# The next layer's modulation steps moved out of the early gates into the background list

## The chip, the cores and the metric

The kernel runs on one core of one Trainium2 chip. The metric is the device time of one execution in microseconds; the time of a kernel is the median of several runs.

## The reference

The model is a trunk of two layers on 512 tokens of width 1024, in float32. Each layer first makes its modulation from the conditioning vector, then runs three token mixers side by side (MLA with 8 heads, a sliding window of 128 with 8 heads, and a differential attention with 4 heads), and merges them by sigmoid gates:

```python
mod = c_act @ w_ada[l] + b_ada[l]
shift, scale, gate = split_cols(mod, (D, D, D))
h = rms_norm(x, g_pre[l]) * (1.0 + scale) + shift
... = split_cols(h @ w_in[l], IN_SPLITS)
o_a, o_b, o_c = (mixer(...) * silu(z)) @ w_o      # MLA, sliding, differential
y = (g[0] * o_a + g[1] * o_b + g[2] * o_c) @ w_out[l]
x = x + gate * rms_norm(y, g_post[l])
```

`mod` does not depend on `x`. So the shift and scale of layer 1 can be computed at any time in layer 0, up to the point where layer 1's `h` is made, and the gate of a layer at any time up to its last line.

## The kernel before

All of the activations stay on the core, transposed (`hTh`, `hTl`: width on the partitions, 512 tokens along the free dimension). Each float32 operand is split into a high part and a remainder, and each product is three matmuls (`mm3`, L87 to L89). A weight block of 128 x 1024 is a unit (`wunit`): one load of 512 KB into `wr` (two buffers), the high part by ACT into `wh` (L81), the remainder by DVE into `wl` (L84), three buffers each. A unit gives 24 matmuls of 128x512 and an accumulator in the PSUM tag `dn` (two buffers).

A layer runs through these stages: MLA's inputs and its eight heads; the early gates (`gates_early`: six gate projections of the second mixer and five of the third, whose units are pulled forward so that their matmuls fill PE during MLA); keys, values and queries of the sliding attention (`swa_kv`, `swa_q`, with the evacuation at L807); the sliding attention (scores at L878 and L879, reductions at L880); four projections for z (`silu_z`); the first merge (eight steps, each with a gate projection and half a unit of `w_o_mla`); the differential attention, head by head (`diff_qkv`, z, scores at L952 and L953, reductions at L954), with the second merge's steps mixed in by `fill`; the third merge; and the output phase, in whose end `boundary_tok` makes the next layer's `h`. The helper `transposed_block` (L704) turns the softmax weights for the products with v.

The modulation of layer 1 is `mod_late`: four quarters of four steps each. A step loads two rows of 512 columns per partition (512 KB into a `wr` buffer, L245) and adds them into an accumulator `acc` with two vector operations (L248 for the first of a quarter, L251 for the others). When a quarter's four steps are through, four products with a column of ones sum the accumulator over the partitions (L257, in `dn`), and one or two small vector operations write `ashf` or `amul`. The gate row of the current layer is `mod_rows`: eight steps, each one load (L229) and one vector operation of 128x1024 (L232, L235). `gate_rows` uses the result at L298 to L302.

Where the steps stand in the program is set by two lists. `some(at)` is called in `gates_early` and `swa_q`; at the positions in `MPOS` it issues one of the first eight steps of `mod_late`. Of the positions, 5, 11 and 12 occur in `gates_early`; a loop after `swa_q` issues the five that are left. What remains of `mod_late`, and then `mod_rows`, is the generator `background`, from which `bg_step` takes one step at a time: after each of the four z projections (`ZBS` is 1), at the start of each step of the first two merges, and twice in each head's `diff_qkv`. `gate_rows` empties what is left.

The final order on each engine is not the program's. A planner orders each engine's queue by priority with modelled durations, where the program's place is the priority and `high_priority` moves instructions up (the units by `WOFF`, 4000 in the early gates and 2000 after them). Each engine then works its queue in that order and waits on semaphores. Buffers of a tag go round: a new tile waits until an older one of its tag is released. The accumulators of the first two quarters take buffers of `u` (eight, shared with the split outputs of the mixers), the other two take `big` (eight).

Of the kernel before, what the change touches and what calls it, by code (L numbers as in the profile page):

```python
# [17 lines left out]
P = 128  # L18
S = 512
# [31 lines left out]
def hybrid_kernel(ctx, tc, x, c, w_ada, b_ada, g_pre, g_post, w_in, g_q, w_uq, g_kv, w_ukv,  # L51
# [11 lines left out]
    def T(tag, shape, dt=F32, bufs=None):  # L63
        count[0] += 1
        return sb.tile(shape, dt, tag=tag, name=f"{tag}_{count[0]}",
                       bufs=bufs or BUFS.get(tag, 1))
# [6 lines left out]
    def Q(tag):  # L73
        count[0] += 1
        return ps.tile([P, S], F32, tag=tag, name=f"ps_{tag}_{count[0]}", bufs=PB[tag])
# [10 lines left out]
    def mm3(o, ah, al, bh, bl, start, stop):  # L86
        pe.matmul(o, ah, bh, start=start, stop=False)  # L87
        pe.matmul(o, ah, bl, start=False, stop=False)  # L88
        pe.matmul(o, al, bh, start=False, stop=stop)  # L89
# [3 lines left out]
    @contextmanager  # L93
    def behind(*ins):
        with ExitStack() as es:
            for i in ins or fence:
                es.enter_context(tc.issue_after(i.ins))
            yield
# [3 lines left out]
    def wunit(parts, big=False):  # L102
        raw = T("wr", [P, 1024])
        h = T("big" if big else "wh", [P, 1024], F32R)
        lw = T("big" if big else "wl", [P, 1024], F32R)
        n = parts[-1][1]
        with tc.high_priority(offset=WOFF[0]):
            for lo, hi, src, shp in parts:
                dst = raw[:, lo:hi]
                if shp:  # L110
                    dst = dst.rearrange("p (a b) -> p a b", a=shp)
                units.append(sp.dma_start(out=dst, in_=src))
            with behind():
                act_copy(h[:, :n], raw[:, :n])
                sub(lw[:, :n], raw[:, :n], f(h[:, :n]))
        return h, lw
# [58 lines left out]
    def par(l, k, i=0, n=1):  # L175
        lo = k + l * PR_STEP[k] + i
        return prT[lo // 32][:, lo % 32:lo % 32 + n]
# [61 lines left out]
    def mod_late(l):  # L239
        for q in range(4):  # L240
            which, j = q // 2, 4 * (q % 2)
            acc = T("u" if q < 2 else "big", [P, S])
            for k in range(0, KT, 2):
                raw = T("wr", [P, 2, S])
                sp.dma_start(out=raw, in_=w_ada[l].rearrange("(p k) b -> p k b", k=KT)  # L245
                             [:, k:k + 2, q * S:(q + 1) * S])
                if k == 0:
                    dve.tensor_scalar(out=acc, in0=raw[:, 0], scalar1=cact[:, 0:1],  # L248
                                      scalar2=None, op0=ALU.mult)
                for i in range(k == 0, 2):  # L250
                    dve.scalar_tensor_tensor(out=acc, in0=raw[:, i],  # L251
                                             scalar=cact[:, k + i:k + i + 1], in1=acc,
                                             op0=ALU.mult, op1=ALU.add)
                yield
            pst = Q("dn")
            for i in range(4):
                pe.matmul(pst[:, i:i + 1], acc[:, i * P:(i + 1) * P], ones[:, 0:1],  # L257
                          start=True, stop=True)
            js = slice(j, j + 4)
            if which == 0:  # L260
                dve.tensor_tensor(out=ashf[l][:, js], in0=pst[:, 0:4],
                                  in1=par(l, PR_SHIFT, j, 4), op=ALU.add)
            else:
                dve.scalar_tensor_tensor(out=amul[l][:, js], in0=pst[:, 0:4], scalar=1.0,
                                         in1=par(l, PR_SCALE, j, 4),
                                         op0=ALU.add, op1=ALU.add)
                dve.tensor_tensor(out=amul[l][:, js], in0=amul[l][:, js],
                                  in1=par(l, PR_GPRE, j, 4), op=ALU.mult)
# [203 lines left out]
    def silu_z(l, col, hh, hl):  # L472
        zz = T("zz", [P, S])
        z = proj_T(l, col, hh, hl)
        return silu_of(zz, z)

    def silu_of(zz, z):
        act.activation(out=zz, in_=z, func=AF.Tanh, scale=0.5)
        dve.scalar_tensor_tensor(out=zz, in0=zz, scalar=1.0, in1=z, op0=ALU.add, op1=ALU.mult)  # L479
        return zz  # L480
# [17 lines left out]
    NC_LATE = 3  # L498
    FN = 1

    MPOS = (5, 6, 7, 8, 9, 10, 11, 12)
    ZBS = 1

    def gates_early(l, hh, hl, some):
        for j in range(NB_EARLY):
            d = dr.tile([P, S], F32, tag=f"gb{l}_{j}", name=f"gb{l}_{j}", bufs=1)
            early[l, 1, j] = d
            t = gate_tanh(l, 1, j, hh, hl)
            act.dma_start(out=d, in_=t)
            some(j)  # L510
        for j in range(NC_LATE, KT):
            d = dr.tile([P, S], F32, tag=f"gc{l}_{j}", name=f"gc{l}_{j}", bufs=1)
            early[l, 2, j] = d
            t = gate_tanh(l, 2, j, hh, hl)
            act.dma_start(out=d, in_=t)
            some(8 + j)
# [278 lines left out]
    def gate_u(o, zz):  # L795
        dve.scalar_tensor_tensor(out=o, in0=o, scalar=0.5, in1=zz, op0=ALU.mult, op1=ALU.mult)
        return split_u(o)
# [47 lines left out]
    def swa_q(l, hh, hl, some):  # L845
        qs = []
        for i in range(4):
            some(16 + i)
            qs += stack_q(l, C_QB + i * P, hh, hl)
        return qs  # L850
# [219 lines left out]
    def rest_of_layer(l, hh, hl, acc, za):  # L1070
        rest = None
        if l == 0:
            fence[:] = [amuls[-1]]
            wh, wl = wunit([(0, 1024, w_in[l][:, C_ZA + 3 * P:C_ZA + 4 * P]
                             .rearrange("(k p) c -> p k c", p=P), KT)])
            z3 = Q("dn")

            def part(lo, hi):
                for k in range(lo, hi):
                    mm3(z3, wh[:, k * P:(k + 1) * P], wl[:, k * P:(k + 1) * P], hh[:, k],  # L1080
                        hl[:, k], k == 0, k == KT - 1)

            def rest(t, ins):
                with behind(ins):
                    part(*ZR[t:t + 2])
                if t == NT - 1:
                    za.append(silu_of(T("zz", [P, S]), z3))

            part(0, ZR[0])
        else:  # L1090
            za = za + [silu_z(l, C_ZA + i * P, hh, hl) for i in range(4)]
        if l == 0:
            fence[:] = [amuls[2]]
        wts = {0: mla_pair_weights(l, 0, "ta")}
        cl, kp = mla_inputs(l, acc, rest)
        v = mla_v(l, cl)
        if l == 0:
            fence.clear()
        oa = mla_attention(l, cl, kp, v, wts)
        tables = [setup_bias()] if l == 0 else []  # L1100
        for t in tables:
            next(t)
        WOFF[0] = 4000
        fence.clear()
        late = mod_late(l + 1) if l + 1 < DEPTH else iter(())
        spread = [8]

        def table():
            if tables:
                try:  # L1110
                    tables[0].send(units[-1])
                except StopIteration:
                    tables.clear()

        def some(at):
            table()
            if at in MPOS and spread[0] > 0:
                spread[0] -= 1
                next(late, None)

        gates_early(l, hh, hl, some)
        WOFF[0] = 2000
        kk, vb = swa_kv(l, hh, hl)
        qs = swa_q(l, hh, hl, some)
        while spread[0] > 0:
            some(MPOS[0])
        for _ in range(12):
            table()
        ua = [gate_u(oa[i], za[i]) for i in range(4)]
        m = []  # L1130
        ob = swa_attention(l, qs, kk, vb)
        bg[:] = [background(l, late)]
        zb = []
        for i in range(4):
            zb.append(silu_z(l, C_ZB + i * P, hh, hl))
            bg_step(ZBS)
        ub = [gate_u(ob[i], zb[i]) for i in range(4)]
        merge(l, 0, w_o_mla, ua, hh, hl, m)
        mb = merge_steps(l, 1, w_o_swa, ub, hh, hl, m, None)
        od = diff_attention(l, hh, hl, lambda n: [next(mb) for _ in range(n)])  # L1140
        for _ in mb:
            pass
        t4 = gates_late(l, hh, hl)
        gg = gate_rows(l)
        return merge(l, 2, w_o_diff, od, hh, hl, m, t4=t4), gg

    hh, hl, acc, za = layer0_input()
    with behind(loads[-1]):
        setup_small()
    for l in range(DEPTH):  # L1150
        if l > 0:
            acc = acc4(True)
# [67 lines left out]
```

## Time and profile before

| | before |
|---|---|
| median of 3 runs | 1180.55 us (1180.5 to 1180.76) |
| the profiled execution's own time | 1178.78 us |
| its span, first to last instruction | 1176.7 us |
| PE busy | 1146.0 us, 97% |
| DVE busy | 844.2 us, 72% |
| ACT busy | 631.5 us, 54% |
| mean granted TensorE clock | 0.993 |

PE is TensorE's matmul queue, DVE VectorE, ACT ScalarE, POOL GpSimd, SP the engine that issues the loads (SPq where the issue itself is meant). A row of the waits gives the engine and line that waited, what it waited for, and the sum, count and longest in us. A row of the timeline gives start and duration in us, engine, line, operation, tiles and shapes; behind it stands the idle time before it, with what ended it. L12 is line 12 of the kernel.

### The profile page before, as it was taken

How to read it: one execution, taken by the hardware profiler on the slowest of the kernel's cores; microseconds unless marked ns; L12 is line 12 of the kernel's file. 1: busy time of each engine (PE TensorE's matmuls, PEld its weight loads, DVE VectorE, ACT ScalarE, POOL GpSimd, SP SyncE). 2: the span in 40 equal slices, each digit the busy share in tenths (PEclk: the TensorE clock that was granted, in tenths of full speed). 3: DMA queues.
4: the chain of work that ended last, by engine and by line, in shares of the span. 5: the costliest groups of instructions: out<-in, count | busy, mean ns of one | idle time of the engine just before them, and what ended most of it. 6: DMA issues, size and time to landing. Idle time of an engine off the chain costs nothing.

```text
span 1176.7 us, 15536 instructions
## 1 busy us (share of the span) xinstructions
PE 1146.0 (97%) x5428; PEld 946.0 (80%) x5428; DVE 844.2 (72%) x1754; ACT 631.5 (54%) x1250; POOL 181.3 (15%) x226
## 2 busy tenths in 40 slices
PE   5899999999999999999999999999999999999997
PEld 4768788878887888888888888888888888888886
DVE  7956686898866687876577567688786568786654
ACT  5355464655543457664357456565564346675432
POOL 4310212122210010101211011222121001100120
PEclk9899999999999999999999999999999999999999
DMA  9537532256355433433454432324533333334442
GB/s 340 190 92 217 186 106 76 72 145 186 108 141 164 110 81 87 117 107 126 143 184 135 114 108 75 86 52 123 157 97 92 95 95 96 88 99 115 136 159 92
DMA packets 169522, 146.86 MB, mean 125 GB/s; under 512 B 7679, under 2 KB 146999, under 8 KB 169444
## 3 DMA queue, kind: packets, MB, share of 16 engines
q1 hardware_dynamic: 166148, 140.08, 40.9%
q10 hardware_dynamic: 3168, 5.77, 1.3%
q8 instruction: 43, 0.70, 0.2%
q14 instruction: 35, 0.29, 0.1%
q0 software_dynamic: 128, 0.01, 0.0%
HBM read 135.83 MB, written 14.20 MB: 127 GB/s over the span
## 4 chain that ended last, share of the span: by engine, by line
PE 84%; DVE 6%; DMA 3%; issue 3%; ACT 1%; POOL 1%; SPq 0%; DVEq 0%; POOLq 0%; ACTq 0%
PE ps_dn L87 20%; PE ps_dn L89 20%; PE ps_dn L88 19%; PE ps_tr L704 5%; PE ps_sc L89 2%; PE ps_sc L87 2%; PE ps_sc L88 2%; PE ps_av L714 1%; PE ps_av L713 1%; PE ps_sc L952 1%; PE ps_sc L953 1%; DMA wr<-in_w_in 1%; DVE o L206 1%; PE ps_pj L87 1%; PE ps_pj L88 1%
## 5 line engine op out<-in xcount | busy, mean ns | idle before, releaser
L87 PE MATMUL ps_dn<-hTh,wh 128*128 128x512 f32 x840 | 331.8, 395 | 1.4 <-DVE zz L479 0.8
L89 PE MATMUL ps_dn<-hTh,wl 128*128 128x512 f32 x840 | 330.5, 393 | 0.4 <-DVE wl L84 0.4
L88 PE MATMUL ps_dn<-hTl,wh 128*128 128x512 f32 x840 | 330.1, 393 | 0.0
L84 DVE TENSOR_TENSOR wl<-wr,wh 128x1024 fp32r<-128x1024 f32 x141 | 178.9, 1269 | 98.5 <-ACT wh L81 97.5
L81 ACT ACTIVATE wh<-wr 128x1024 fp32r<-128x1024 f32 x141 | 149.1, 1058 | 162.7 <-PE ps_dn L88 111.2
L87 PEld LDWEIGHTS ps_dn<-hTh,wh 128*128 128x128 f32 x840 | 158.2, 188 | 33.2 <-PE ps_dn L89 1.0
L89 PEld LDWEIGHTS ps_dn<-hTh,wl 128*128 128x128 f32 x840 | 158.0, 188 | 33.3 <-DVE wl L84 0.9
L88 PEld LDWEIGHTS ps_dn<-hTl,wh 128*128 128x128 f32 x840 | 158.1, 188 | 31.7
L84 DVE TENSOR_TENSOR pt<-ps_tr,pt 128x512 fp32r<-128x512 f32 x136 | 92.2, 684 | 30.5 <-ACT pt L81 29.6
L81 ACT ACTIVATE pt<-ps_tr 128x512 fp32r<-128x512 f32 x136 | 78.8, 596 | 64.8 <-PE ps_tr L704 63.6
L775 POOL TENSOR_SCALAR p<-p,st 128x512 f32<-128x512 f32 x64 | 52.2, 834 | 279.3 <-DVE st L773 243.7
L704 PE MATMUL ps_tr<-ident,p 128*128 128x128 f32 x544 | 92.4, 273 | 0.9 <-POOL p L775 0.6
L704 PEld LDWEIGHTS ps_tr<-ident,p 128*128 128x128 f32 x544 | 69.5, 141 | 20.2 <-POOL p L775 1.8
L87 PE MATMUL ps_dn<-u,wh 128*128 128x512 f32 x192 | 75.9, 395 | 0.0
L89 PE MATMUL ps_dn<-u,wl 128*128 128x512 f32 x192 | 75.9, 395 | 0.0
L88 PE MATMUL ps_dn<-u,wh 128*128 128x512 f32 x192 | 75.2, 391 | 0.0
L963 POOL TENSOR_SCALAR ta<-ta,st 128x512 f32<-128x512 f32 x32 | 26.7, 834 | 306.9 <-ACT wh L81 143.1
L894 POOL TENSOR_SCALAR p<-p,st 128x256 f32<-128x256 f32 (+1 forms) x64 | 42.1, 676 | 157.7 <-DVE st L892 130.4
L771 ACT ACTIVATE p<-ps_sc,st 128x512 f32<-128x512 f32 x64 | 43.7, 685 | 28.0 <-DVE st L770 27.7
L770 DVE TENSOR_REDUCE st<-ps_sc 128x1 f32<-128x512 f32 x64 | 43.4, 686 | 21.3 <-PE ps_sc L89 20.8
L886 ACT ACTIVATE p<-p,st 128x256 f32<-128x256 f32 (+1 forms) x64 | 35.7, 558 | 21.9 <-DVE st L884 21.2
L959 ACT ACTIVATE p<-p,st 128x512 f32<-128x512 f32 x32 | 23.1, 723 | 38.8 <-DVE st L957 38.7
(345 smaller groups left out, 2100.5 us busy)
## 6 DMA issues: line engine op xcount, KB each, us to landing
wr<-in_w_in SPq DMA_DIRECT2D x105, 512.0 KB, 3.7
wr<-in_w_ada SPq DMA_DIRECT2D x32, 512.0 KB, 3.6
wr<-in_w_out SPq DMA_DIRECT2D x16, 512.0 KB, 3.6
big<-in_w_ada SPq DMA_DIRECT2D x10, 512.0 KB, 7.6
big<-in_x SPq DMA_DIRECT2D x8, 512.0 KB, 5.3
wr<-in_w_o_mla SPq DMA_DIRECT2D x8, 512.0 KB, 4.0
wr<-in_w_o_swa SPq DMA_DIRECT2D x8, 512.0 KB, 3.4
wr<-in_w_o_diff SPq DMA_DIRECT2D x8, 512.0 KB, 3.7
```

The costliest lines, as they stand in the source:

```text
L81: return act.activation(out=out_, in_=in_, func=AF.Copy, scale=scale)
L84: return (eng or dve).tensor_tensor(out=out_, in0=a, in1=b, op=ALU.subtract)
L87: pe.matmul(o, ah, bh, start=start, stop=False)
L88: pe.matmul(o, ah, bl, start=False, stop=False)
L89: pe.matmul(o, al, bh, start=False, stop=stop)
L704: pe.transpose(tr[:, i * P:(i + 1) * P], b, ident)
L770: dve.tensor_reduce(out=nm[:, t:t + 1], in_=s, axis=AX.X, op=ALU.max, negate=True)
L771: act.activation(out=pr[:, t], in_=s, func=AF.Exp, bias=nm[:, t:t + 1], accum_out=sm[:, t:t + 1])
L775: pool.tensor_scalar(out=pr[:, t], in0=pr[:, t], scalar1=rr[:, t:t + 1], scalar2=1.0, op0=ALU.mult, op1=ALU.mult)
L886: act.activation(out=pr[:, i, :w], in_=pr[:, i, :w], func=AF.Exp, bias=nm[:, i:i + 1], accum_out=sm[:, i:i + 1])
L894: pool.tensor_scalar(out=pr[:, i, :w], in0=pr[:, i, :w], scalar1=rr[:, i:i + 1], scalar2=1.0, op0=ALU.mult, op1=ALU.mult)
L963: pool.tensor_scalar(out=pc[1], in0=pc[1], scalar1=rr[:, 1:2], scalar2=1.0, op0=ALU.mult, op1=ALU.mult)
```

## The change

Two edits place all sixteen steps of `mod_late` in the background list: `MPOS` becomes empty, so that `some` issues none, and the loop that issued the rest after `swa_q` is taken out. A third puts the accumulators of the first two quarters into `big` like the others. The steps themselves, their loads, their vector operations and the column sums are the same in number and size. The background list of layer 0 has 24 steps where it had 16; that of layer 1, where there is no next layer, has eight as before.

```diff
     def mod_late(l):
         for q in range(4):
             which, j = q // 2, 4 * (q % 2)
-            acc = T("u" if q < 2 else "big", [P, S])
+            acc = T("big", [P, S])
             for k in range(0, KT, 2):
...
-    MPOS = (5, 6, 7, 8, 9, 10, 11, 12)
+    MPOS = ()
     ZBS = 1
...
         kk, vb = swa_kv(l, hh, hl)
         qs = swa_q(l, hh, hl, some)
-        while spread[0] > 0:
-            some(MPOS[0])
         for _ in range(12):
             table()
```

## The prediction

> **What bounds the kernel now.** I read the page's busy line first, then the waits of PE (TensorE's matmuls), then stretches of the span side by side, then the queues of PE, DVE and SP inside the stretch that stood out.
>
> ```profile
> span 1176.7 us, 15536 instructions
> PE 1146.0 (97%) x5428; PEld 946.0 (80%) x5428; DVE 844.2 (72%) x1754; ACT 631.5 (54%) x1250; POOL 181.3 (15%) x226
> ```
>
> PE is busy for 1146.0 of 1176.7 us. The change takes no matmul away and adds none, so only PE's idle time and the clock under its matmuls can move. Between the start and the tail, PE's waits are few:
>
> ```profile
> PE ps_sc L878 <- DVE st L880: 1.1, 1, 1.1
> PE ps_av L713 <- DVE st L884: 0.9, 1, 0.9
> ...
> PE ps_dn L87 <- DVE op L807: 0.6, 1, 0.6
> PE ps_tr L704 <- POOL p L775: 0.6, 2, 0.3
> ```
>
> All four lie in layer 0, where the modulation steps run. The first two are the hand-over from MLA to the sliding attention. The columns of the next view are the stretch and its length, then busy time (x instructions) of PE, PEld, DVE, ACT, POOL, the granted clock, the DMA share and GB/s:
>
> ```profile
> 210.00:220.00 10.00, 10.00 (x53) 8.28 (x52) 9.86 (x16) 7.61 (x15) 3.38 (x4) 1.00 0.19 53
> 220.00:230.00 10.00, 10.00 (x50) 8.15 (x49) 9.78 (x16) 5.87 (x12) 0.00 (x0) 1.00 0.34 107
> 230.00:240.00 10.00, 10.00 (x52) 8.12 (x51) 9.84 (x15) 4.60 (x10) 3.77 (x4) 1.00 0.42 117
> 240.00:249.10 9.10, 6.96 (x42) 5.33 (x40) 8.73 (x21) 4.90 (x9) 0.64 (x1) 1.00 0.71 184
> 249.10:253.50 4.40, 4.40 (x14) 3.42 (x15) 4.31 (x9) 3.97 (x10) 0.00 (x0) 0.61 0.40 111
> ...
> 400.00:500.00 100.00, 100.00 (x474) 82.42 (x473) 82.55 (x200) 63.64 (x117) 11.26 (x15) 1.00 0.36 96
> ```
>
> From 210 to 240 DVE is 98% busy while PE is still full; at 240 to 249.1 PE loses 9.10 - 6.96 = 2.14 us, and right after it the clock is 0.61 for 4.40 us, which costs 4.40 x (1 - 0.61) = 1.72 us more. The stall is worth 2.14 + 1.72 = **3.86 us**. What DVE does then, and what PE gets:
>
> ```profile
> 245.46 0.48 DVE L248 TENSOR_SCALAR big<-wr,cact 128x512 f32<-128x512 f32 x1
> 245.98 0.75 DVE L251 SCALAR_TENSOR_TENSOR big<-wr,cact,big 128x512 f32<-128x512 f32 x1
> 246.65 0.48 DVE L880 CUSTOM_DVE_ANT_0 p<-ps_sc,x,sinkt 128x256 f32<-128x256 f32 x1
> ```
>
> ```profile
> 244.31 0.95 PE L257 MATMUL ps_dn<-ones,u 128*128 128x1 f32 x8
> 245.40 0.66 PE L704 MATMUL ps_tr<-ident,p 128*128 128x128 f32 x4
> 247.19 0.39 PE L878 MATMUL ps_sc<-op,op 128*128 128x256 f32 x1 [1.13 <-DVE st L880]
> ...
> 249.08 0.61 PE L713 MATMUL ps_av<-pt,big 128*128 128x512 f32 x1 [0.87 <-DVE st L884]
> ```
>
> L880, which frees the score's PSUM buffer, runs at 246.65 with two modulation operations just before it, and L878 starts once it is done. PE has no projection to run meanwhile, and the load queue shows why:
>
> ```profile
> 175.22 21.75 SPq L112 DMA_DIRECT2D wr<-in_w_in  x3
> ...
> 211.62 23.43 SPq L245 DMA_DIRECT2D wr<-in_w_ada  x5
> 237.99 0.37 SPq L112 DMA_DIRECT2D wr<-in_w_in  x1
> 241.60 0.37 SPq L245 DMA_DIRECT2D wr<-in_w_ada  x1
> 244.65 0.37 SPq L112 DMA_DIRECT2D wr<-in_w_in  x1
> ```
>
> The two `wr` buffers take loads in the order of the program. Five modulation loads stand together between the last of three weight loads (175.22 + 21.75 = 197.0) and the next at 237.99. So no weights come in for 41 us, and PE's stock of filler runs out.
>
> **The change, part by part.** The eight moved steps are four loads of 512 KB and eight vector operations for each of two quarters:
>
> ```profile
> L251 DVE SCALAR_TENSOR_TENSOR u<-wr,cact,u x14: 710/751/1175, 105.7 to 240.8; 128x512 f32<-128x512 f32 x14
> L251 DVE SCALAR_TENSOR_TENSOR big<-wr,cact,big x14: 736/744/914, 246.0 to 298.7; 128x512 f32<-128x512 f32 x14
> L235 DVE SCALAR_TENSOR_TENSOR big<-wr,cact,big x14: 1275/1284/1477, 323.9 to 859.3; 128x1024 f32<-128x1024 f32 x14
> ```
>
> 1. *Taken from 101 to 241 us.* 14 operations of 0.75 us and two first ones of 0.48 (the L248 row above) are 11.5 us of DVE, plus eight loads on SP. Gain: the stall, 3.86 us, if what comes in their place does not stall too. Lower bound 0. For an upper bound I use layer 1, which runs the same stages without these steps:
>
> ```profile
> 112.90:386.71 273.81, 270.31 (x1318) 221.41 (x1317) 211.99 (x423) 147.33 (x305) 47.49 (x64) 0.99 0.46 132
> 684.11:947.87 263.76, 263.76 (x1288) 217.15 (x1287) 192.73 (x389) 147.13 (x305) 46.78 (x64) 1.00 0.36 99
> ```
>
> Both run from an MLA score matmul to the first differential one: layer 1 needs 10.05 us less and PE never idles. Of these, the column sums stay: eight matmuls in 0.95 us (the L257 row), 32 in all, so 3.8 us. That leaves 10.05 - 3.8 = 6.2, or 5.6 without the 0.64 us of point 3. I take 3.86, the part whose rows I can point at; 5.6 stays as the bound.
>
> 2. *Put behind the sliding attention, steps 1 to 16.* There the list now holds these eight first, then the eight that were there. Per step 2 x 0.744 = 1.49 us against 1.28 for a row step: 0.2 x 8 = 1.6 us more DVE where eight row steps ran, spread over 70 us. Layer 1 already has steps at the same places (its row steps), and there, at the hand-over, DVE is 36.78 of 40.40 us busy and PE full:
>
> ```profile
> 781.60:822.00 40.40, 40.40 (x205) 33.12 (x204) 36.78 (x66) 24.67 (x51) 9.02 (x12) 1.00 0.38 105
> ```
>
> I cost it at nothing. The cover is filler in time; without it the 3.86 come back.
>
> 3. *Row steps, now 17 to 24, pushed into the differential attention.* The list is called four times by the z weights, eight by the first merge and four by the first two heads. So the last eight fall between heads 0 and 3, which is the stretch of 400 to 500 us in the table, give or take 10 us. That is 7 x 1.284 + 0.75 = 9.7 us of DVE into a stretch where it is 82.55 of 100 us busy: about 92%. Their eight SP issues (the L245 rows: 0.37 us each) are queued ahead of the weight loads of these heads: 11 of those, so 19 loads in some 90 us, one per 4.7 us, while the queue above takes one per 3 to 4 us (237.99, 241.60, 244.65). Price of a collision, from the one that is there today:
>
> ```profile
> 378.31 0.68 DVE L807 SCALAR_TENSOR_TENSOR op<-ps_dn,op 64x512 fp32r<-64x512 f32 x1
> 379.03 1.28 DVE L235 SCALAR_TENSOR_TENSOR big<-wr,cact,big 128x1024 f32<-128x1024 f32 x1
> 380.34 0.69 DVE L807 SCALAR_TENSOR_TENSOR op<-ps_dn,op 64x512 fp32r<-64x512 f32 x1
> ```
>
> ```profile
> 381.18 0.47 PE L87 MATMUL ps_dn<-hTh,wh 128*128 128x512 f32 x1 [0.64 <-DVE op L807]
> ```
>
> A row step got between two evacuations of a q projection, and the next projection waited 0.64 us for its PSUM buffer (two modulation halves at that place after the change can do the same). Bounds for eight moved steps: 0, and 8 x 0.64 = 5.1 us with one half-clock stretch of 1.72 on top, 6.8. I take one collision, **+0.64**, since the 16 row steps of both layers have made one such wait.
>
> 4. *Buffers and sums.* The two accumulators go from `u` to `big`, and the later ones shift: four merge tiles, the last accumulator, two v tiles and the gate accumulator make the eight of `big`, so the third head's v waits for the last column sum, issued just before. Also the planner that writes the queues' order starts from another list, so every order after 101 us may differ; the rows can't show that. Bounds for both: 0.64 either way; taken 0. The gate row is wanted late:
>
> ```profile
> L300 PE MATMUL ps_sc<-pt,onesr x4: 389/389/389, 543.1 to 1104.8; 128*128 128x512 f32 x4
> ```
>
> Its last step moves from 379.03 to some 100 us later, still 60 us ahead of 543.1. The two 0.3 us waits for POOL early in MLA may go with the three early steps; I count 0, bound 0.6 of gain.
>
> Sum: -3.86 + 0.64 = **-3.2 us**. Against the profiled execution (1178.78 us, span 1176.7) that is 1175.6; the median of 1180.55 lies 1.77 above it, so **1177.3**.
>
> The Trainium skill, in "TensorE: Matmul & The Clock Gate", section "Why this matters for your kernels", wants idle gaps of more than about 3 us before the clock drops. Here two gaps of 1.13 and 0.87 us, with transposes and one-column matmuls between, were followed by 0.61, so I go by the trace; by the rule the clock's 1.72 us would not hang on the stall, and the time would be 1179.1.
>
> **Rivals.**
>
> *B, layer 0 walks like layer 1.* Point 1 gives the whole 5.6 us and point 3 costs nothing: 1180.55 - 5.6 = 1174.9. For it: the same stages in the same file at a full PE. Against: point 3 has no twin in layer 1.
>
> *C, the steps do not go where the change says.* Loads follow program order through `wr`, and the first background steps stand right behind the first z load, which now closes the 41 us hole. Four steps (4 x 1.49 = 6 us of DVE) then land in 210 to 250 in place of 8.4 us (five steps and the 0.48 + 0.75 of a sixth, one of the ten being a first one of 0.48), DVE stays near 95%, and the stall moves by some us or is cut in half: 0 to -1.9, with the 0.64 about 1180.2. For it: DVE is 98% busy there, of which steps are only a fifth (8.4 of 39). Against: weights keep coming between the steps, and layer 1 bore 91%.
>
> *D, slower.* The row steps block the differential attention. DVE works in order; a step whose load is late holds up the score reductions and the evacuations behind it, and ACT's exponentials and PE behind those.
>
> ```profile
>   DVE big L235: 7.2, 9
> ```
>
> Row steps waited for their load nine times, 0.8 us each. 9.7 + 8 x 0.8 = 16 us on 82.55 would be over 98%; the point from which it decides is DVE past 96%, as at 240 to 249.1. Then all eight cost 0.64 and one half-clock stretch follows: +6.8 - 3.86 = +3.0, so 1183.5. Against: PE held out at 98% for 30 us above while filler lasted, and here every head brings four projections. The Trainium skill, in the same page's Part 1, speaks for it too: there VectorE's queue is a strict FIFO, which the order of 378.31 to 381.18 agrees with.
>
> **How the numbers follow.** My forecast (a gain of 2.4 to 4.5 us) gets 0.46, B 0.12, C 0.24, D 0.18. Steps of 0.2%, 2.4 us, are about what can be told from no change here. The range goes from 1173.9, the 5.6 us and 1 us for the early waits, to 1181.9, no gain from the stall and two collisions: it leaves out most of D and a bit of B. The forecast's own range is 1176 to 1178.2. Faster is the forecast and B, 0.58; the same is C, 0.24; slower is D, 0.18.
>
> **What would show it.** Right: no modulation load in 101 to 205 us; weight loads without a hole of 41 us between 197 and 238; PE full and clock 1.00 from 230 to 260; the stretch from first MLA score to first differential score near 270 us; DVE at about 92 of 100 in the differential stretch with PE at 99 or more. Wrong: PE idle there again behind L880 (C), or a row of short PE waits behind L807, L954 or L84 between 390 and 480 with a clock under 1.00 (D).

## The result, and the profile after

| | before | after |
|---|---|---|
| median | 1180.55 us (5 runs, 1180.34 to 1180.77) | 1188.43 us (5 runs, 1186.97 to 1190.43) |
| the profiled execution's own time | 1178.78 us | 1189.43 us |
| its span | 1176.7 us | 1187.6 us |
| mean granted TensorE clock | 0.993 | 0.988 |

The ratio is 1.0069, 95% interval 1.0054 to 1.0083: **slower**, by 0.7%. The forecast was 1177.3 with a range to 1181.9, so the result lies outside it on the far side.

The busy line of the kernel after:

```profile
span 1187.6 us, 15554 instructions
...
PE 1151.4 (97%) x5428; PEld 948.4 (80%) x5428; DVE 843.6 (71%) x1754; ACT 628.8 (53%) x1250; POOL 184.2 (16%) x226
```

The number of matmuls is the same (5428). The span of the profiled execution grew by 10.9 us, which the account below splits; the medians differ by 7.9 us. PE's busy time grew by 5.4 us, although it does the same matmuls: most of that is the half clock (at most 5.1 us, by the account below). The other 5.5 us are idle time (1187.6 - 1151.4 = 36.2 against 30.7). DVE is busy no longer than before.

PE's waits after (engine and line, what it waited for; sum, count, longest):

```profile
PE ps_av L714 <- DVE pt L84: 2.2, 1, 2.2
PE ps_tr L704 <- POOL p L894: 2.1, 1, 2.1
PE ps_dn L87 <- DVE big L557: 1.5, 1, 1.5
...
PE ps_dn L87 <- DVE st L957: 1.0, 1, 1.0
...
PE ps_sc L952 <- DVE st L954: 0.7, 1, 0.7
```

None of the four waits that the prediction showed of before is left, and these five are the longest that have come. Stretches of the span after (busy time and instructions of PE, PEld, DVE, ACT, POOL; granted clock; DMA):

```profile
240.00:250.00 10.00, 10.00 (x52) 8.28 (x51) 8.41 (x19) 5.33 (x12) 0.00 (x0) 1.00 0.47 133
250.00:260.00 10.00, 10.00 (x51) 8.40 (x50) 7.26 (x19) 4.42 (x9) 2.32 (x4) 1.00 0.40 107
...
270.00:280.00 10.00, 5.72 (x32) 4.50 (x30) 7.87 (x18) 4.74 (x11) 1.75 (x2) 0.96 0.44 127
...
370.00:380.00 10.00, 8.47 (x27) 6.79 (x27) 5.85 (x11) 2.52 (x4) 0.00 (x0) 0.66 0.58 159
...
400.00:500.00 100.00, 98.27 (x461) 79.91 (x460) 83.91 (x188) 57.88 (x105) 11.77 (x12) 1.00 0.47 133
```

```profile
279.20:286.00 6.80, 6.12 (x15) 4.47 (x16) 2.21 (x10) 1.09 (x4) 2.15 (x4) 0.50 0.69 208
371.40:378.20 6.80, 6.19 (x15) 4.89 (x16) 4.45 (x8) 1.28 (x3) 0.00 (x0) 0.50 0.68 186
```

The stall at 240 to 253 is gone: PE is full there at full clock. In its place stand two stalls, each followed by 6.8 us at clock 0.50, worth 6.8 x (1 - 0.50) = 3.4 us each. That is an upper value: PE is idle in the first half microsecond of each stretch, and a product of 128x512 starts every 0.43 us in it where one starts every 0.23 us at full clock. The last row of the account, found by difference, is larger by as much as the 3.4 are too large. The account, in us:

| | gain | loss |
|---|---|---|
| stall at 240 to 253 (3.86), early waits for POOL (0.6), wait behind L807 at 381.18 (0.64) | 5.1 | |
| A: 277 to 286, idle 2.18 + 2.10, half clock 3.4 | | 7.7 |
| B: 369 to 378, idle 0.34 + 1.53, half clock 3.4 | | 5.3 |
| C: waits in the differential attention, 0.73 + 1.00 at 419 and 493, 0.56 + 0.27 at 508 | | 2.6 |
| other small waits, by difference to the 10.9 | | 0.4 |

**Stall A**, after. First the load queue: the hole of 41 us is gone, and modulation loads and weight loads take turns.

```profile
208.05 0.37 SPq L112 DMA_DIRECT2D wr<-in_w_in  x1
221.04 0.37 SPq L245 DMA_DIRECT2D wr<-in_w_ada  x1
228.43 0.37 SPq L112 DMA_DIRECT2D wr<-in_w_in  x1
229.56 0.37 SPq L245 DMA_DIRECT2D wr<-in_w_ada  x1
...
270.02 0.37 SPq L112 DMA_DIRECT2D wr<-in_w_in  x1
271.16 0.37 SPq L245 DMA_DIRECT2D wr<-in_w_ada  x1
```

```profile
273.51 0.15 DVE L888 TENSOR_TENSOR st<-sinkt,st 128x4 f32<-128x4 f32 x1
275.76 0.75 DVE L251 SCALAR_TENSOR_TENSOR big<-wr,cact,big 128x512 f32<-128x512 f32 x1 [2.10 <-DMA wr<-in_w_ada]
276.43 0.68 DVE L84 TENSOR_TENSOR pt<-ps_tr,pt 128x512 fp32r<-128x512 f32 x1
...
277.88 0.18 DVE L892 RECIPROCAL st<-st 128x4 f32<-128x4 f32 x1
...
279.13 0.68 DVE L479 SCALAR_TENSOR_TENSOR zz<-zz,ps_dn 128x512 f32<-128x512 f32 x1
...
280.54 0.15 DVE L261 TENSOR_TENSOR ashf<-ps_dn,prT 128x4 f32<-128x4 f32 x1
```

```profile
278.25 3.10 POOL L894 TENSOR_SCALAR p<-p,st 128x384 f32<-128x384 f32 x4 [10.79 <-DVE st L892]
```

```profile
272.29 0.72 PE L257 MATMUL ps_dn<-ones,big 128*128 128x1 f32 x6
...
274.70 0.28 PE L257 MATMUL ps_dn<-ones,big 128*128 128x1 f32 x2
277.17 0.45 PE L714 MATMUL ps_av<-pt,big 128*64 128x512 f32 x1 [2.18 <-DVE pt L84]
279.72 1.60 PE L704 MATMUL ps_tr<-ident,p 128*128 128x128 f32 x3 [2.10 <-POOL p L894]
280.97 0.78 PE L87 MATMUL ps_dn<-hTh,wh 128*128 128x512 f32 x1
```

The modulation load is issued at 271.16, when its `wr` buffer comes free; its operation L251 stands at the head of DVE's queue, and DVE does nothing for 2.10 us. Behind it wait the split L84, for which PE's L714 waits, and the reciprocal L892, for which POOL's scaling and then PE's transposes wait. A projection had no `dn` buffer to run in, for both were taken: one held the finished z projection, whose evacuation L479 also waited in DVE's queue and began only at 279.13; the other held a column sum, whose eight products ran from 272.29 to 274.98 and which L261 read only at 280.54. No wait row of PE names `dn` here: in PE's queue the next projection (280.97) stands behind L714 and L704, in the order that the planner wrote. That the buffer made it so is an inference, which **sumpj**, below, bears out: there the same projections stand ahead of the waiting transposes. So two waits of some 2 us reach PE without any filler.

**Stall B**, after:

```profile
367.84 1.06 ACT L81 ACTIVATE wh<-wr 128x1024 fp32r<-128x1024 f32 x1 [7.26 <-PE ps_dn L89]
368.80 0.58 ACT L492 ACTIVATE tf<-ps_dn 128x512 f32<-128x512 f32 x1
```

```profile
369.43 1.05 PE L257 MATMUL ps_dn<-ones,big 128*128 128x1 f32 x8 [0.34 <-ACT tf L492]
372.01 0.80 PE L87 MATMUL ps_dn<-hTh,wh 128*128 128x512 f32 x1 [1.53 <-DVE big L557]
```

The sum of the third quarter stands at the thirteenth call of the background list, between the first merge's last product and the first q projection of the differential attention. It takes the `dn` buffer that L492 frees, so the q projection must wait for the merge's own evacuation, L557 (371.27 to 371.95). Before, there was no sum at that place, and the projection took that buffer itself.

### The profile page after: what moved, and what is told of

It reads as the page before. It is cut to its first block, busy times and chain, and to the rows that moved or that the text cites. A ratio compares the mean times of both kernels' runs of the same rounds, so it can differ in the third digit from the quotient of the medians.

```text
span 1187.6 us, 15554 instructions
## 1 busy us (share of the span) xinstructions
PE 1151.4 (97%) x5428; PEld 948.4 (80%) x5428; DVE 843.6 (71%) x1754; ACT 628.8 (53%) x1250; POOL 184.2 (16%) x226
## 4 chain that ended last, share of the span: by engine, by line
PE 57%; DVE 3%; DMA 2%; issue 1%; ACT 1%; POOL 1%; DVEq 0%; POOLq 0%; SPq 0%; ACTq 0%
PE ps_dn L87 14%; PE ps_dn L88 14%; PE ps_dn L89 13%; PE ps_tr L704 3%; PE ps_sc L89 1%; PE ps_sc L87 1%; PE ps_sc L88 1%; PE ps_sc L952 1%; PE ps_sc L953 1%; PE ps_av L87 1%; PE ps_av L88 1%; PE ps_av L89 1%; DMA wr<-in_w_out 1%; PE ps_pj L87 1%; PE ps_av L714 1%
## 5 line engine op out<-in xcount | busy, mean ns | idle before, releaser
L84 DVE TENSOR_TENSOR wl<-wr,wh 128x1024 fp32r<-128x1024 f32 x141 | 179.4, 1273 | 116.7 <-ACT wh L81 116.0
L84 DVE TENSOR_TENSOR pt<-ps_tr,pt 128x512 fp32r<-128x512 f32 x136 | 92.3, 685 | 22.5 <-ACT pt L81 21.5
L704 PE MATMUL ps_tr<-ident,p 128*128 128x128 f32 x544 | 92.9, 273 | 2.8 <-POOL p L894 2.1
L704 PEld LDWEIGHTS ps_tr<-ident,p 128*128 128x128 f32 x544 | 69.9, 141 | 22.5 <-POOL p L894 3.2
L963 POOL TENSOR_SCALAR ta<-ta,st 128x512 f32<-128x512 f32 x32 | 29.5, 921 | 314.0 <-ACT wh L81 75.4
```

The source lines that it names most:

```text
L84: return (eng or dve).tensor_tensor(out=out_, in0=a, in1=b, op=ALU.subtract)
L704: pe.transpose(tr[:, i * P:(i + 1) * P], b, ident)
L963: pool.tensor_scalar(out=pc[1], in0=pc[1], scalar1=rr[:, 1:2], scalar2=1.0, op0=ALU.mult, op1=ALU.mult)
```

## The experiments

Each ratio is against the kernel before, timed on the same chip. The runs were on several chips, so the ratios are to be compared, more than the times. A profile shows one execution, whose time can differ from the median. Expectations stand as they were written before each run.

### One edit of the change, or part of it

**tags**: the kernel before, with the third edit alone.

```diff
-            acc = T("u" if q < 2 else "big", [P, S])
+            acc = T("big", [P, S])
```

> The kernel before with one of the three edits alone: the accumulators of the first two quarters in big instead of u; the steps stay where they were. If the buffers have a part in the loss, the time rises by over 1 us, by H and R alone it stays at 1180.5 within 1 us. Theory S: any such edit rewrites the order and moves the time by 2 us or more, either way.

Measured: 1185.10 us, ratio 1.0041 (1.0022 to 1.0060). The edit that was costed at nothing costs some 5 us alone. In its profile the stall near 245 is larger (idle 0.66 + 2.85, where it was 1.13 + 0.87, and 3.4 us of half clock as before) and a second one has come, with the same rows as stall A and 3.4 us of half clock:

```profile
284.05 0.75 DVE L251 SCALAR_TENSOR_TENSOR big<-wr,cact,big 128x512 f32<-128x512 f32 x1 [2.39 <-DMA wr<-in_w_ada]
284.72 0.68 DVE L84 TENSOR_TENSOR pt<-ps_tr,pt 128x512 fp32r<-128x512 f32 x1
```

```profile
288.01 0.33 PE L704 MATMUL ps_tr<-ident,p 128*128 128x128 f32 x1 [2.10 <-POOL p L894]
```

**five**: the kernel after, with the three steps of the early gates kept there and only the five of the cluster moved.

```diff
-    MPOS = ()
+    MPOS = (5, 11, 12)
...
-        spread = [8]
+        spread = [3]
```

> Only the five steps after the sliding queries are moved; the three among the early gates stay (accumulators in big). The column sums then stand at the second, sixth, tenth and fourteenth background call, so none stands at the hand-over from the first merge to the differential attention. Theory P: no stall near 370 us. Theory H: the loads in the sliding attention are the same as in the changed kernel, so a stall near 280 us is likely. Together 1180 to 1184 us. If each moved step costs its share, 5/8 of the loss: 1185.4. Theory S: anything between 1178 and 1190.

Measured: 1181.38 us, ratio 1.0011 (1.0000 to 1.0022). With three steps fewer in the list, the sums come three calls earlier, at no hand-over. In the profiled execution, the fastest of ten (1178.78 us), neither stall A nor stall B appears, one wait of 1.06 us at 263.2 is a projection waiting for a sum's reader (L261), and the clock stays at full speed from 100 us to the tail.

### What in a step makes the stalls

**noload** and **loadonly**: the kernel after, once without the sixteen loads (the operations read another tile), once with the loads but only one operation per quarter.

```diff
-                raw = T("wr", [P, 2, S])
-                sp.dma_start(out=raw, in_=w_ada[l].rearrange("(p k) b -> p k b", k=KT)
-                             [:, k:k + 2, q * S:(q + 1) * S])
...
-                    dve.scalar_tensor_tensor(out=acc, in0=raw[:, i],
+                    dve.scalar_tensor_tensor(out=acc, in0=rq,
```

```diff
-                for i in range(k == 0, 2):
-                    dve.scalar_tensor_tensor(out=acc, in0=raw[:, i],
-                                             scalar=cact[:, k + i:k + i + 1], in1=acc,
-                                             op0=ALU.mult, op1=ALU.add)
```

> The changed kernel without the sixteen loads of the next layer's steps: their vector operations stay in place and read the resident rope table, so layer 1's shift and scale are made from other data. Theory H (VectorE, working in order, waits 15.2 us for these loads, and PE loses 5 us idle and 5 us at half clock behind it): the two stalls at 277 and 369 us go, about 1177 us. Theory W (the work itself, 1.49 us of VectorE per step, is too much in its new place): the stalls stay, about 1188. Theory S (the planner's new order is unlucky, whatever moved): a time anywhere between 1178 and 1186, with PE waits at other places.

> The changed kernel with all sixteen loads but only the first vector operation of each quarter: 28 vector operations are left out, so layer 1's shift and scale are incomplete. Theory H: four operations are left that can wait, so most of the loss goes, 1177 to 1181 us. Theory R (the steps hold one of the two wr buffers, so weights come late, whatever VectorE does): a load without a reader frees its buffer on landing some 3.7 us after its issue, where a step held it 6 to 11 us, so a part stays, 1182 to 1186. Theory W: 1176 to 1178. Theory S: 1178 to 1186 with waits at other places.

Measured: noload 1181.31 us, ratio 1.0018 (1.0009 to 1.0028); loadonly 1179.16 us, ratio 1.0001 (0.9992 to 1.0011). Stall A is gone from both: it needs the load and the operation that waits for it in DVE's queue. Stall B is in both (waits of 1.58 and 1.13 us for the merge's evacuation near 365, each with a half clock of 3.4 us), so it hangs neither on the loads nor on the operations. Both keep the column sums (and the longer list and the third edit). In noload theory H is missed, which asked for 1177 us and for both stalls to go, and so is theory W with 1188; loadonly lies in theory H's 1177 to 1181.

**onpool**: the kernel after, with the steps' operations on GpSimd.

```diff
-                    dve.scalar_tensor_tensor(out=acc, in0=raw[:, i],
...
+                    pool.tensor_scalar(out=raw[:, i], in0=raw[:, i], scalar1=cact[:, k + i:k + i + 1],
+                                       scalar2=1.0, op0=ALU.mult, op1=ALU.mult)
+                    pool.tensor_tensor(out=acc, in0=acc, in1=raw[:, i], op=ALU.add)
```

> The changed kernel with the steps' vector operations on GpSimd (a scaling in place and an addition in place of the one fused operation, about 0.83 and 1.1 us each). The waits for the loads move to a queue that PE depends on only through the softmax scalings. Theory H: VectorE's waits for these loads fall from 15 us to near 0 and the time to 1177 to 1181 us. Theory R: buffers are held longer than before, 4 us of GpSimd per step, so 1188 or more. Theory S: 1180 to 1188 with waits at other places.

Measured: 1190.39 us, ratio 1.0096 (1.0080 to 1.0111). The wait moved with the operation. POOL's queue in that run:

```profile
277.43 1.36 POOL L252 TENSOR_SCALAR wr<-wr,cact 128x512 f32<-128x512 f32 x2 [4.54 <-DMA wr<-in_w_ada]
278.77 2.27 POOL L895 TENSOR_SCALAR p<-p,st 128x384 f32<-128x384 f32 x4
```

The scaling of the softmax weights stands behind the late step as the split stood before, and PE's transposes waited 4.05 us in one piece.

**lag**: the kernel after, with each step's operations issued one call after its load, so that the load has landed when DVE comes to them. The column sums come one call later with them.

```diff
+                for t in todo:
+                    t()
+                todo[:] = [lambda a=acc, r=raw, k=k: ops(a, r, k)]
                 yield
...
```

> The changed kernel with each step's vector operations issued one background call after its load, so that the load has landed when VectorE comes to them. Nothing is left out. Theory H (VectorE stands at a load that is under way, with the softmax tiles' evacuation behind it): the first stall, 4.3 us idle and 3.4 us of lost clock around 280 us, goes, 1180 to 1182 us, and VectorE's waits for these loads fall from 15 us to under 4. Theory R (a step holds one of two wr buffers): it is held longer now, weights come later, 1188 to 1194. Theory S (the planner's order is a lottery): 1178 to 1190, with the DVE waits no guide to it.

Measured: 1198.20 us, ratio 1.0151 (1.0131 to 1.0171), the slowest of all. DVE's waits for these loads fell from 15.2 us to 5.2, as meant, but the step now keeps one of the two `wr` buffers while it lags, and weights come late:

```profile
PE ps_dn L87 <- ACT wh L81: 4.0, 2, 3.2
```

This is theory R's direction, beyond its 1188 to 1194; theory H is missed. The granted clock was 0.50 for 17.1 us between 100 us and the tail, against 13.7 us in the kernel after. Since the order of all queues and the place of the sums changed too, how much of the loss is the buffer held back from the weights is not shown.

**norows**: the kernel after without layer 0's eight gate-row steps.

```diff
+        if l == 0:
+            for hf in range(2):
+                dve.tensor_scalar(out=acc[:, hf * S:(hf + 1) * S], in0=rq, scalar1=cact[:, 0:1],
+                                  scalar2=None, op0=ALU.mult)
+            for k in range(KT):
+                yield acc
+            return
```

> The changed kernel without the eight steps of layer 0's gate row: no loads and no operations for it, one multiplication of the rope table fills the accumulator, so layer 0's gate comes out of other data. Theory N (the row steps in the differential attention make the small waits at 419, 493 and 508 us, 2.6 us together): these go, 1185 to 1186 us, the stalls at 277 and 370 stay. If the small waits come from the new order there, and not from the steps, the time stays at 1188 within 1 us.

Measured: 1183.10 us, ratio 1.0030 (1.0014 to 1.0045), its executions spread from 1180.83 to 1186.66. In the profiled execution (1181.16 us) the gaps of stalls A and B stay (2.06 + 1.86, and 1.53), but the half clock behind B is absent; of the waits C only one of 0.39 is left:

```profile
400.00:500.00 100.00, 99.61 (x472) 81.74 (x471) 83.20 (x202) 62.61 (x117) 11.18 (x14) 1.00 0.33 91
```

PE is at 99.61 of 100 us there, against 98.27. So the waits C go with the row steps. The time is some 2 us below theory N's 1185 to 1186: in this execution the 3.4 us of half clock behind stall B are gone too, which the theory did not foresee.

### The column sums

**sumlate**: the kernel after, with the sums of the first three quarters one background call later.

```diff
+                for t in todo:
+                    t()
+                todo.clear()
+            todo.append(lambda a=acc, w=q // 2, j=4 * (q % 2): sums(a, w, j))
```

> The changed kernel with the column sums of the first three quarters issued one background call later. That of the third then stands between the first differential head's q and k projections and no longer ahead of the q projection, where it takes one of the two PSUM buffers that the merge's last product still holds the other of. Theory P (that is the second stall: 1.9 us idle and 3.4 us of lost clock at 369 to 378 us): it goes, about 1183 us, and the first stall at 277 stays. If the second stall has to do with late weights or with the loads instead, the time stays at 1188.

Measured: 1181.21 us, ratio 1.0011 (1.0001 to 1.0020). No half clock is left between 100 us and the tail. Stall B went, as theory P said, and stall A went with it, which no theory said. DVE waits for the load as long as in the kernel after:

```profile
275.45 0.75 DVE L247 SCALAR_TENSOR_TENSOR big<-wr,cact,big 128x512 f32<-128x512 f32 x1 [2.08 <-DMA wr<-in_w_ada]
```

But PE runs projections meanwhile and loses 0.95 and 0.27 us there. So the wait in DVE's queue is not enough for stall A; the sum in `dn` has to come to it.

**sumpj** tests that directly: the sums stay where they are and only take another PSUM tag, `pj`, whose one buffer the projections at stalls A and B do not use.

```diff
-            pst = Q("dn")
+            pst = Q("pj")
```

> The changed kernel with one word altered: the column sums of the modulation go to the PSUM tag pj (one buffer) in place of dn (two buffers). Number, size and place of all steps stay. Theory P (a column sum waiting in one of the two dn buffers keeps the projections, which fill PE, from running): the stall at 277 to 286 and the one at 369 to 378 lose their half-clock stretches (6.8 us each at half speed, 3.4 us lost each) and their longest gaps, PE's idle time after 100 us falls from 9.45 us to 4 to 6, and the time is 1180 to 1183. Theory H (VectorE at the head of its queue waiting for a modulation load is the whole loss): the 2.1 us wait of L251 or L247 near 275 stays with its gaps and half clock, and the time is 1186 to 1190. Theory S (what moves the time is only the new order of all queues): no forecast, and the gaps would be at places that have nothing to do with the sums.

Measured: 1178.86 us, ratio 0.9994 (0.9984 to 1.0003). **One word takes back the whole loss.** The queue of DVE still shows the late load, and PE still waits once for POOL:

```profile
277.45 0.75 DVE L251 SCALAR_TENSOR_TENSOR big<-wr,cact,big 128x512 f32<-128x512 f32 x1 [1.67 <-DMA wr<-in_w_ada]
```

```profile
277.15 0.39 PE L87 MATMUL ps_dn<-hTh,wh 128*128 128x512 f32 x1
...
277.83 0.39 PE L87 MATMUL ps_dn<-hTh,wh 128*128 128x512 f32 x1
...
280.77 0.33 PE L704 MATMUL ps_tr<-ident,p 128*128 128x128 f32 x1 [2.09 <-POOL p L894]
```

The first gap of stall A is filled with projections, the second (2.09) stays with a half clock of 3.4 us in place of 6.8; stall B is a wait of 0.53 without one. PE's idle time from 100 to 1150 us falls from 9.64 to 4.99 us. That is theory P's size, and a little better than its 1180 to 1183; theory H fails, since DVE's waits for these loads are still 10.2 us of 15.2.

**bsumpj** and **tagspj**: the same word in the kernel before, and in **tags**.

> The kernel before with the column sums in pj in place of dn, nothing else. There the sums stand at 244.31 (eight matmuls of one column, just ahead of the two gaps of 1.13 and 0.87 us). Theory P: a projection gets the dn buffer sooner, the stall of 3.86 us shrinks by 1 to 3.9, time 1176.5 to 1179.5. Theory H with the missing weight loads (no load for 41 us, so there is no projection to run whichever buffer is free): the stall stays and the time is 1180 to 1181.5.

> The kernel before with the accumulators of the first two quarters in big (the change's third edit, which alone gave the ratio 1.0041) and the column sums in pj. Theory P2: the loss of the third edit is paid through the dn buffer that a column sum holds as well, at the waits near 245 to 250 and 285 to 288; then it goes, and the time is that of the kernel before with the sums in pj, ratio 0.998 to 1.000. Theory S: the loss comes from the new order of the queues and has nothing to do with the sums; then the ratio stays at 1.003 to 1.005.

Measured: bsumpj 1178.46 us, ratio 0.9988 (0.9979 to 0.9998); tagspj 1178.16 us, ratio 0.9991 (0.9982 to 1.0000). In tagspj the 0.41% of the third edit are gone: it was paid through `dn` too, not by the new order as such. How another buffer for the accumulators leads to waits in `dn` is not shown. In bsumpj the old stall at 240 to 253 is gone, though its cluster of five loads stands where it stood:

```profile
196.83 0.37 SPq L112 DMA_DIRECT2D wr<-in_w_in  x1
211.86 23.44 SPq L245 DMA_DIRECT2D wr<-in_w_ada  x5
238.84 0.37 SPq L112 DMA_DIRECT2D wr<-in_w_in  x1
```

```profile
240.00:250.00 10.00, 9.99 (x54) 8.11 (x53) 8.61 (x19) 5.49 (x9) 1.07 (x1) 1.00 0.75 205
250.00:260.00 10.00, 9.85 (x52) 7.95 (x51) 7.75 (x20) 4.93 (x14) 0.00 (x0) 1.00 0.45 115
```

42 us without a weight load, and PE is full all the same. Part of the gain is given back by a wait of 1.54 us at 288. With the sums in `pj` the kernels before and after cannot be told apart (0.9988 and 0.9994, with overlapping intervals), so the move itself then gains nothing that shows.

**spread**, **spreadpj** and **spread2pj**: the kernel before with the eight early steps one at a time; the last two with the sums in `pj`.

```diff
-    MPOS = (5, 6, 7, 8, 9, 10, 11, 12)
+    MPOS = (5, 11, 12, 13, 14, 15, 16, 17)
```

In spread2pj the positions are (11, 12, 13, 14, 15, 16, 17, 18).

> The kernel before with its first eight steps kept ahead of the sliding attention, but spread: one each at three positions of the early gates and one each at five positions of the sliding queries, so that the five that stood together after the queries are gone; tags and background list as before. If the cluster of five loads (41 us without a weight load) is the cause of the stall at 240 to 253, that stall goes and the time is 1176 to 1178.5. If the steps themselves load VectorE too much wherever they stand, a stall appears 20 to 40 us earlier instead and the time is 1180 to 1184.

> The same spread kernel with the column sums in pj. Theory P: not slower than spread, and up to 1.5 us faster, by the 0.64 us wait near 381 and by a free dn buffer at the hand-over near 245: 1175 to 1178. If sums in dn matter only together with a late load, it equals spread within 1 us.

> The kernel before with its eight early steps one at each of eight positions, the last five of the early gates and the first three of the sliding queries, and the sums in pj. The step at the earlier position 5 is gone from there, and with it the waits for GpSimd at 131 to 134, if that step makes them (0.7 us before, 1.9 us with a half-clock stretch of 3.4 us in the spread kernels). Then 1174.5 to 1177, ratio 0.996 to 0.998. If these waits come from the steps at the later positions or from the order alone, the ratio is that of the other spread kernel, 0.998.

Measured: spread 1183.61 us, ratio 1.0029 (1.0018 to 1.0039); spreadpj 1177.80 us, 0.9982 (0.9972 to 0.9991); spread2pj 1177.57 us, 0.9982 (0.9972 to 0.9991). The spread was a miss for both theories: the stall at 245 went, no stall came 20 to 40 us earlier, but one came 40 us later, again just behind a sum in `dn`, with 6.8 us of half clock (and the waits for POOL at 131 to 134 grew from 0.6 to 1.9 us, with 3.4 us of half clock):

```profile
281.77 0.95 PE L257 MATMUL ps_dn<-ones,big 128*128 128x1 f32 x8
...
286.49 0.58 PE L878 MATMUL ps_sc<-op,op 128*128 128x256 f32 x1 [2.17 <-DVE st L880]
```

With `pj` it loses 1.12 us at that place and no clock, while the waits near 134 stay as in spread. In spread2pj the waits at 131 to 134 are gone as well, and its profiled span is the shortest of all (1174.0 us), but its median cannot be told from spreadpj's, so what these waits are worth stays open (the profiled execution of spread2pj was the fastest of its ten, that of spreadpj the slowest). Both beat the kernel before and the kernel after, by some 0.2%.

**fivepj**: **five** with the sums in `pj`.

> The changed kernel with three early steps kept ahead of the sliding attention (only five moved) and the sums in pj. With the sums in dn the ratio was 1.0011, and there no sum stood at a hand-over. Theory P: the sums cost little there, so the ratio falls by 0.1% at most, to 1.000 or 1.001. If each sum costs a buffer wait wherever it stands, it falls to 0.997 to 0.999.

Measured: 1179.58 us, ratio 1.0005 (0.9995 to 1.0015), within theory P. The intervals of five and fivepj overlap: where the sums stand at no hand-over, their tag matters little.

The tag of the sums also changes the order that the planner writes, so a single pair could be chance. Three pairs went the same way with intervals far apart: 1.0069 to 0.9994, 1.0041 to 0.9991, 1.0029 to 0.9982. The kernel before went to 0.9988, and five, with no sum at a hand-over, from 1.0011 to 1.0005, inside the intervals.

## Why the prediction was wrong

**What bounds the kernel now.** The stall at 240 to 253 was seen and sized rightly, and its cause was half wrong. I wrote that PE's stock of filler runs out because no weights come in for 41 us. In bsumpj the hole is the same and the stall is gone. The kernel before shows it too. The unit loaded at 237.99 was split and ready at 244.63, ahead of both gaps, yet PE's next projection began at 251.48:

```profile
243.40 1.23 DVE L84 TENSOR_TENSOR wl<-wr,wh 128x1024 fp32r<-128x1024 f32 x1
```

```profile
251.48 0.78 PE L87 MATMUL ps_dn<-hTh,wh 128*128 128x512 f32 x1
```

The row that mattered was quoted in the prediction: L257 at 244.31, eight one-column products in `dn`, just ahead of both gaps. I used it for its 0.95 us of PE time and not for the buffer it takes.

**Step 1, the stall goes: right in size.** Gained were the 3.86 us, the 0.6 of the early waits for POOL (counted at 0 with a bound of 0.6) and the 0.64 at 381: 5.1 us. Without the 0.64, which rival B's 5.6 leaves out, it is 4.5, between the 3.86 taken and that bound. The column sum at 244.31 left this place together with the steps, so that the stall went does not bear out the reason given for it.

**Step 2, steps 1 to 16 cost nothing: failed, up to 7.7 us (stall A).** It leaned on layer 1, which has steps at the same places with PE full. But those are row steps: they have no column sums in `dn`. The twin was the right place to look and lacked the one thing that counted. The cover named there, filler in time, was in memory; it had no PSUM buffer to run in. Part of the 7.7 may belong to step 4: in tags, where no step moved, a smaller stall with the same rows came at 285 to 293. No run moves the steps with the accumulators left in `u`, so the split stays open. The mechanism of rival D (a step whose load is late blocks DVE's queue) is what starts the stall, but in the sliding attention, where D did not put it, and by sumlate and sumpj it costs little when the sums are out of the way. D's point of decision, DVE past 96%, was wrong too. Two stretches of the differential attention after:

```profile
440.00:450.00 10.00, 10.00 (x49) 8.28 (x48) 9.71 (x20) 4.61 (x9) 1.80 (x2) 1.00 0.49 142
470.00:480.00 10.00, 10.00 (x47) 8.20 (x46) 9.72 (x24) 5.84 (x12) 0.69 (x1) 1.00 0.29 90
```

DVE is at 97% there and PE full; at stall A, DVE was busy for 7.87 of 10 us. What decided was the order in the queue and who held the buffers.

**Step 3, the row steps: mechanism right, size off.** One collision of 0.64 was taken, bounds 0 to 6.8; it came to 2.6 us and no half clock; in norows 0.39 of it is left.

**Step 4, buffers and sums, taken 0 with 0.64 either way: failed.** It named only the `big` tag and the planner's order. The third edit alone costs 0.41% (tags), and stall B, 5.3 us, is a sum that the longer list pushed onto a hand-over. Both are paid in `dn`, of which the step did not speak. The list is eight steps longer, so the sums of the last two quarters move by eight calls and those of the first two come into it; the question to ask was which projection is next in `dn` at each of these calls.

**The clock.** One half-clock stretch, worth 1.72 us, was the most that I allowed; two worth up to 3.4 us each came. Of the 10.9 us more, at most 5.1 are the clock's (2 x 3.4 - 1.72).

**What would show it.** Right: no modulation load before 221.04, no hole of 41 us, PE full and clock 1.00 from 230 to 260. Wrong: first MLA score to first differential score took 279.7 us (111.7 to 391.4), not 270, and PE fell to 98.27 in the differential stretch. The eight row steps came where step 3 put them (414.29 to 482.15), but DVE was busy for 83.91 of 100 us there, not for 92: the stages run some 11 us later by then, and the stretch holds less of the other work (L84 28.16 us, where it was 32.50).

## What to carry to other kernels

When work is moved in program order, follow not only its engine time and its loads but the ring of each buffer that it touches: a tiny product that takes one of two accumulators, and whose reader stands in a busy in-order queue, can hold the accumulator for 8 us (272.29 to 280.54) and take away the filler that hides everything else. Give such small results a PSUM tag that the filler does not use before changing where they stand. A twin stage proves that a move is free only if it has the same tiles in the same rings.

## What the runs showed of the hardware

The granted clock fell to 0.50 after idle gaps that are short one by one. Two gaps of 2.18 and 2.10 us with a single 0.45 us product between, and gaps of 0.34 and 1.53 us with only one-column products between, were each met by 6.8 us at 0.50; before, gaps of 1.13 and 0.87 were met by a single stretch of 3.4 us, which cost 1.72. (The prediction put transposes and one-column products between these two gaps; those stand ahead of the first, and between the two stand four score products, from 247.19 to 248.21.) But for the one that ends each run, the stretches in all of these runs are 3.4, 6.8 or 10.2 us long, and each 3.4 us costs up to 1.7 us. The length of a gap alone does not decide: in sumpj a gap of 2.09 us was followed by 3.4 us at half clock, in loadonly one of 1.13 us by 3.4 us, in bsumpj one of 1.54 us by none, and the 1.53 us of stall B by 6.8 us in the kernel after (with 0.34 just ahead) and by none in norows. What decides is not shown. The Trainium skill, in "TensorE: Matmul & The Clock Gate", section "A second HAM failure mode: psum-queue depth-cycling", tells of a kernel whose clock swung because TensorE idled briefly and often between groups of matmuls; these rows agree with that more than with the gap of about 3 us that the prediction weighed.
